# Even tokens first in every block, side taps of one chain alone, and a gate projected feature by token

## The chip, the cores and the metric

The kernel runs on one core of a Trainium2 chip. The metric is device time in microseconds (us) of one execution, from input in HBM to output in HBM. Engines are named as in the profile: PE is TensorE (matmuls; PEld its weight loads), DVE VectorE, ACT ScalarE, POOL GpSimd, SP SyncE, which issues all DMAs here.

## The reference

2048 tokens of 1024 features pass two residual layers and a last RMSNorm. Layer 0 is gated linear attention with 4 heads in chunks of 64 tokens, layer 1 a causal convolution module with 31 taps per channel. Each has a gate path z that multiplies the layer's output before its output projection. All is float32.

```python
def gla_mixer(h, w_in, w_g2, b_g, gn_w, w_out):          # layer 0
    q, k, v, z, g_lr = split(h @ w_in)
    log_a = log_sigmoid(g_lr @ w_g2 + b_g) / 16
    o = gla_chunked(q * dk**-0.5, k, v, log_a)            # state S, 64 tokens at a time
    o = o * rsqrt(mean(o * o) + EPS) * gn_w               # per head of 256
    return (o * silu(z)) @ w_out

def conv_mixer(h, w_in, dw_w, dw_b, ln_w, ln_b, w_out):   # layer 1
    a, gl, z = split(h @ w_in)
    u = causal_depthwise_conv(a * sigmoid(gl), dw_w) + dw_b   # 31 taps
    u = silu(layernorm(u, ln_w, ln_b))
    return (u * silu(z)) @ w_out

x = x + gla_mixer(rmsnorm(x), ...); x = x + conv_mixer(rmsnorm(x), ...); return rmsnorm(x)
```

## The kernel before

Work goes by two halves of 1024 tokens (`hf`), each in two blocks of 512 (`b`). Data lie with features on the 128 partitions and tokens along them. Every projection is three matmuls for one (`mm3`, L139 to 145): both operands are split into a high and a low part (`ah`/`al` for activations, `wh`/`wl` for weights, which ACT and POOL split in L124 and L125 as each unit of 256 columns arrives), and high x high, high x low and low x high are summed in a bank of PSUM. `proj_f` (L147) keeps 128 weight columns stationary and moves 512 tokens, so its result lies feature by token. `proj_t` (L152) keeps 128 tokens stationary and moves 256 weight columns, so its result lies token by feature. Eight row blocks make 24 matmuls in either.

Layer 0 (`head`, L442) goes head by head: q and k, the values v, then eight steps `i` of 128 tokens. A step projects z with `proj_t`, applies Silu on ACT (L472), and runs three parts of `core`: scores, `mix` (the output `o`, the state S) and `turn`. In `mix` the sum of squares gives a factor `ss`, and DVE multiplies o, ss and z into g (L403). `turn` transposes g back to feature by token on PE (L413); ACT copies it with the norm's weight (L418), and SP stores 256 tokens of it, read again by the output projection (`out1`).

Layer 1 (`in2`) projects a, gate and z of every unit. `glu` writes u = a * sigmoid(gate), with even tokens in `u[:, 0]` and odd ones in `u[:, 1]` (L754, a write in steps). `conv` splits the 31 taps into three filters of half length: A is 16 taps on even tokens, B 15 on odd ones, C 16 on even + odd. Even outputs are A plus B one token late, odd ones C - A - B, so 47 taps of 512 tokens stand for 62. On DVE a chain of taps is one multiply-add each (L638) into a bank of PSUM; its first tap also takes in what came before (L640 for C, L642 for A and B). The first `nside` taps of A and as many of B are done beside DVE: ACT multiplies (L622), POOL adds (L624). `SIDES` gives `nside` for each of eight chunks of 128 channels in both halves. POOL (in the first half) or DVE (in the second) forms even + odd in place (L669) once A is done. `even` (L647), `odd` (L652) and `sums` (L659) make the outputs and the sum for the layer norm. A layer norm of one half runs beside the projections of the next or beside `out2`, which adds the output projection to x (L838), sums squares (L844), scales (L864) and stores.

The order on each engine comes from a scheduler that plans with its own time line. The code sets priorities (`PRIO`), and `pump` (L588) doles out the list of conv and layer norm steps between projections. Pools set what waits: PSUM has three banks `mm` for projections, two `pb` for chains, three `pm`. Each engine works its queue in order.

Of the kernel before, what the change touches and what calls it, by code (L numbers as in the profile page):

```python
# [13 lines left out]
P = 128  # L14
# [16 lines left out]
SIDES = ((1, 7, 7, 7, 7, 5, 9, 7),  # L31
         (1, 5, 3, 5, 9, 7, 6, 4))
# [8 lines left out]
def kernel(  # L41
    ctx: ExitStack,
    tc: tile.TileContext,
    xT: bass.AP,
    wall: bass.AP,
# [21 lines left out]
    ps_m = ctx.enter_context(tc.tile_pool(name="ps_m", bufs=3, space=bass.MemoryType.PSUM))  # L67

# [70 lines left out]
    def mm3(ps, terms):  # L139
        n = len(terms)  # L140
        i = 0
        for sh, sl, mh, ml in terms:
            for s, m in ((sh, mh), (sh, ml), (sl, mh)):
                pe.matmul(ps, s, m, start=(i == 0), stop=(i == 3 * n - 1))  # L144
                i += 1

    def proj_f(ps, w, c0, a):  # L147

        wh, wl = w
        mm3(ps, [(wh[:, k, c0:c0 + P], wl[:, k, c0:c0 + P], a[k][0], a[k][1]) for k in range(KT)])  # L150
# [75 lines left out]
    wgr = l1c.tile([P, KT, 16], F32, name="wgr")  # L226

    masks = l1c.tile([P, 192], I32, name="masks")
# [9 lines left out]
    def load_small():  # L238
        sp.dma_start(out=wgr, in_=wg)
# [41 lines left out]
    def gate_low(hf, b, a, acc):  # L281
# [14 lines left out]
        rbs = t2("tmp")  # L296
        act.activation(rbs[0:96], rb[0:96], AF.Copy)
        gv = t2("tmp")
        dve.tensor_tensor(gv[0:96], ps[0:96], rbs[0:96], ALU.mult)
# [58 lines left out]
    late = []  # L358

# [5 lines left out]
    def core(hf, h, i, v, sz, qkb, sink):  # L365
# [11 lines left out]
        def scores():  # L377
# [3 lines left out]
            dve.copy_predicated(st[CK:P, CK:P], masks[CK:P, P:P + CK], s_ps[CK:P, P:P + CK])  # L381
# [3 lines left out]
        def mix():  # L385
# [17 lines left out]
            dve.scalar_tensor_tensor(g, o_ps, ss, sz, ALU.mult, ALU.mult)  # L403
            sink["g", i] = g

        def turn():
# [4 lines left out]
            for c in range(2):  # L411
                o = c * 256 + (i % 2) * P
                pe.transpose(gt[:, o:o + P], g[:, c * P:(c + 1) * P], ident)  # L413
            if i % 2 == 1:
                st = t2("st")
                for c in range(2):
                    cs = slice(c * 256, (c + 1) * 256)
                    act.activation(st[:, cs], gt[:, cs], AF.Copy, scale=cc(C_GN, 2 * h + c))  # L418
                if h < HEADS - 1:
                    for c in range(2):  # L420
                        r0 = (2 * h + c) * P
                        sp.dma_start(
                            out=gd[hf, r0:r0 + P, (i - 1) * P:(i + 1) * P],
                            in_=st[:, c * 256:(c + 1) * 256])
                else:
                    sink["stage"].append(st)
# [15 lines left out]
    def head(hf, h, a, EEs, g3s, stage):  # L442
# [23 lines left out]
        sink = {"stage": stage}  # L466
        todo = []
        for i in range(8):
            ps = mm_bank()[:, 0:DV]
            proj_t(ps, w, a[i // 4], i % 4)  # L470
            sz = l1p.tile([P, DV], F32, name="sz", bufs=3)
            act.activation(sz, ps, AF.Silu, scale=rt[:, hf * 8 + i:hf * 8 + i + 1])  # L472
            todo.append(core(hf, h, i, vs[i], sz, qkb[i // 4], sink))
# [20 lines left out]
    def out1(hf, stage, ahead):  # L494
        a = [[], []]
        for b in range(2):
            if b == 1:
                run_late(0)
            for k in range(KT):
# [6 lines left out]
                else:  # L506
                    for s in range(2):
                        src = stage[b * 2 + s][:, (k - 6) * 256:(k - 5) * 256]
                        ds = slice(s * 256, (s + 1) * 256)
                        act.activation(hi[:, ds], src, AF.Copy)  # L510
                        dve.tensor_tensor(lo[:, ds], src, hi[:, ds].bitcast(F32), ALU.subtract)
                a[b].append((hi, lo))
        accs = [l1p.tile([P, NB], F32, name="acc", bufs=2) for _ in range(2)]
        for pair in range(2):
            ws = [next_unit(12 + 2 * pair), next_unit(13 + 2 * pair)]
            for b in range(2):
                t0 = hf * TH + b * NB
                for ch in range(4 * pair, 4 * pair + 4):
                    xr = l1p.tile([P, 4, 3, CK], F32, name="Q", bufs=2).rearrange("p a b c -> p (a b c)")[:, 0:NB]
                    sp.dma_start(out=xr, in_=xT[ch * P:(ch + 1) * P, t0:t0 + NB])  # L520
# [77 lines left out]
    def conv(hf, c, u, dst, S1):  # L598
# [13 lines left out]
        def side(which):  # L612

            st[which] = l2p.tile([P, NB + 1], F32, name="conv" + which, bufs=2)
            acc = st["p" + which] = st[which][:, 1:NB + 1]
            for m in range(nside):
                src, w = tap(which, m)
                p = acc if m == 0 else l2p.tile([P, NB], F32, name="prod", bufs=2)
                if m == 0 and which == "B":
                    act.activation(p, src, AF.Identity, scale=w, bias=cc(C_DWB, c))  # L620
                else:
                    act.activation(p, src, AF.Copy, scale=w)  # L622
# [3 lines left out]
        def chain(which, m0, m1, n):  # L626
            def fn():
                first = 0 if which == "C" else nside
                if m0 == first:
                    st["ps"] = b_bank()  # L630
                ps = st["ps"]
# [19 lines left out]
        def odd():  # L651
            dve.scalar_tensor_tensor(  # L652
                dst[c][:, 1], st["ps"], dwb2[:, c:c + 1], st["B"][:, 1:NB + 1], ALU.add, ALU.subtract)
# [8 lines left out]
        for which, n in (("A", 16), ("B", 15), ("C", 16)):  # L662
            m0 = 0 if which == "C" else nside
# [324 lines left out]
```

## Time and profile before

| | |
|---|---|
| median of 3 runs | 1676.16 us (1675.92 to 1680.72) |
| profiled execution | 1678.1 us, span 1676.0 us |
| granted clock of PE, mean | 0.983 |
| PE, DVE, POOL, ACT busy | 96%, 58%, 54%, 44% of the span |
| DMA | 165.68 MB, 99 GB/s |

The span runs from the first to the last instruction in the trace. Layer 0 takes the first 860 us, the conv layer's input projections the time to 1445 us, and the last output projections the rest. Busy times of matmuls overlap, so PE's share is no measure of what it could do: the distance between the starts of two matmuls is. A wait is shown as the idle time before an instruction with what ended it.

### The profile page before, as it was taken

How to read it: one execution, taken by the hardware profiler on the slowest of the kernel's cores; microseconds unless marked ns; L12 is line 12 of the kernel's file. 1: busy time of each engine (PE TensorE's matmuls, PEld its weight loads, DVE VectorE, ACT ScalarE, POOL GpSimd, SP SyncE). 2: the span in 40 equal slices, each digit the busy share in tenths (PEclk: the TensorE clock that was granted, in tenths of full speed). 3: DMA queues.
4: the chain of work that ended last, by engine and by line, in shares of the span. 5: the costliest groups of instructions: out<-in, count | busy, mean ns of one | idle time of the engine just before them, and what ended most of it. 6: DMA issues, size and time to landing. Idle time of an engine off the chain costs nothing.

```text
span 1676.0 us, 23547 instructions
## 1 busy us (share of the span) xinstructions
PE 1609.4 (96%) x9028; PEld 1410.2 (84%) x9028; DVE 972.7 (58%) x1481; ACT 739.6 (44%) x1246; POOL 900.2 (54%) x787
## 2 busy tenths in 40 slices
PE   8999999999999999999999999999999899999697
PEld 6989999998889999999888887877788678877597
DVE  7433232241434232325243999989699999977634
ACT  6645252342557353415232544443553355435432
POOL 4444343334744333323342989985398798456342
PEclk9999999999999999999999999999999999999798
DMA  6021111144511212123452211225154113643633
GB/s 190 26 83 57 64 51 57 57 139 139 169 45 33 82 51 64 45 63 102 144 164 88 76 38 38 94 70 157 59 174 157 57 45 101 202 163 124 234 115 137
DMA packets 74016, 165.68 MB, mean 99 GB/s; under 512 B 7760, under 2 KB 16464, under 8 KB 73904
## 3 DMA queue, kind: packets, MB, share of 16 engines
q1 hardware_dynamic: 73904, 164.19, 30.5%
q8 instruction: 70, 1.15, 0.3%
q14 instruction: 42, 0.34, 0.1%
HBM read 128.51 MB, written 35.65 MB: 98 GB/s over the span
## 4 chain that ended last, share of the span: by engine, by line
PE 73%; DVE 16%; DMA 3%; ACT 3%; issue 2%; POOL 2%; SPq 0%; POOLq 0%; DVEq 0%; ACTq 0%
PE mm L144 63%; DVE pb L638 10%; PE pb L144 3%; PE pb L388 1%; PE pb L390 1%; DVE pb L642 1%; PE pm L379 1%; DMA wr<-in_wall_dram 1%; PE pm L413 1%; DVE u L754 1%; DVE al L190 1%; PE pm L288 1%; POOL acc L205 1%; DMA u<-x_scratch 1%; DVE pb L640 1%
## 5 line engine op out<-in xcount | busy, mean ns | idle before, releaser
L144 PE MATMUL mm<-ah,wh 128*128 128x512 f32 (+1 forms) x1600 | 595.3, 388 | 44.8 <-DVE u L838 20.4
L144 PE MATMUL mm<-al,wh 128*128 128x512 f32 (+1 forms) x1600 | 592.6, 385 | 0.0
L144 PE MATMUL mm<-ah,wl 128*128 128x512 f32 (+1 forms) x1600 | 590.0, 386 | 0.0
L125 POOL TENSOR_TENSOR wl<-wr,wh 128x1024 fp32r<-128x1024 f32 x140 | 344.0, 2471 | 214.9 <-ACT wh L124 208.9
L144 PEld LDWEIGHTS mm<-ah,wh 128*128 128x128 f32 x1600 | 302.3, 190 | 110.1 <-DVE u L838 20.0
L144 PEld LDWEIGHTS mm<-al,wh 128*128 128x128 f32 x1600 | 302.2, 190 | 57.1 <-issue 0.2
L144 PEld LDWEIGHTS mm<-ah,wl 128*128 128x128 f32 x1600 | 301.4, 190 | 58.0 <-issue 0.2
L144 PE MATMUL mm<-wh,ah 128*128 128x256 f32 x896 | 259.2, 289 | 0.0
L144 PE MATMUL mm<-wh,al 128*128 128x256 f32 x896 | 254.7, 284 | 0.0
L144 PE MATMUL mm<-wl,ah 128*128 128x256 f32 x896 | 254.2, 284 | 0.0
L124 ACT ACTIVATE wh<-wr 128x1024 fp32r<-128x1024 f32 x144 | 145.5, 1051 | 140.9 <-PE mm L144 92.4
L638 DVE SCALAR_TENSOR_TENSOR pb<-u,C,pb 128x512 f32<-128x512 f32 x252 | 184.9, 747 | 0.7
L638 DVE SCALAR_TENSOR_TENSOR pb<-u,dwc,pb 128x512 f32<-128x512 f32 x240 | 179.9, 750 | 1.2
L144 PEld LDWEIGHTS mm<-wl,ah 128*128 128x128 f32 x896 | 171.4, 191 | 0.4
L144 PEld LDWEIGHTS mm<-wh,ah 128*128 128x128 f32 x896 | 171.3, 191 | 0.4
L144 PEld LDWEIGHTS mm<-wh,al 128*128 128x128 f32 x896 | 171.3, 191 | 0.0
L622 ACT ACTIVATE prod<-u,C 128x512 f32<-128x512 f32 x148 | 105.5, 721 | 135.7 <-POOL convA L624 68.4
L624 POOL TENSOR_TENSOR convA<-convA,prod 128x512 f32<-128x512 f32 x74 | 98.3, 1329 | 5.7 <-ACT prod L622 1.6
L624 POOL TENSOR_TENSOR convB<-convB,prod 128x512 f32<-128x512 f32 x74 | 98.0, 1325 | 4.0 <-ACT convB L620 0.7
L397 DVE SCALAR_TENSOR_TENSOR S<-S,dec,pb 128x256 f32<-128x256 f32 x56 | 26.8, 479 | 95.4 <-PE pb L144 95.3
L401 POOL TENSOR_TENSOR ss<-ss,e 128x1 f32<-128x1 f32 x64 | 13.4, 209 | 124.4 <-ACT g L400 124.4
L523 DVE TENSOR_TENSOR Q<-mm,Q 128x512 f32<-128x512 f32 x32 | 22.1, 689 | 93.0 <-PE mm L144 78.3
(195 smaller groups left out, 2174.1 us busy)
## 6 DMA issues: line engine op xcount, KB each, us to landing
wr<-in_wall_dram SPq DMA_DIRECT2D x144, 512.0 KB, 4.1
raw<-in_xT_dram SPq DMA_DIRECT2D x32, 256.0 KB, 3.7
Q<-in_xT_dram SPq DMA_DIRECT2D x32, 256.0 KB, 3.2
x_scratch<-Q SPq DMA_DIRECT2D x32, 256.0 KB, 3.1
sz_scratch<-t SPq DMA_DIRECT2D x32, 256.0 KB, 2.3
b<-sz_scratch SPq DMA_DIRECT2D x32, 256.0 KB, 3.5
g_scratch<-st SPq DMA_DIRECT2D x48, 128.0 KB, 1.9
raw<-g_scratch SPq DMA_DIRECT2D x24, 256.0 KB, 3.5
```

Of the source, the lines that this page charges most:

```text
L124: act.activation(wh[:, ks, :], raw, AF.Copy)
L125: (dve if i < 2 else pool).tensor_tensor(wl[:, ks, :], raw, wh[:, ks, :].bitcast(F32), ALU.subtract)
L144: pe.matmul(ps, s, m, start=(i == 0), stop=(i == 3 * n - 1))
L190: dve.tensor_tensor(lo, src, hi.bitcast(F32), ALU.subtract)
L205: eng.tensor_tensor(acc, acc, sq, ALU.add)
L288: pe.matmul(ps, wgs[:, k, :], m, start=(n == 0), stop=(n == 15))
L379: pe.matmul(s_ps[:, 0:192], ki[:, js], Q[:, j].rearrange("p s c -> p (s c)"), start=True, stop=True)
L397: dve.scalar_tensor_tensor(S[h], S[h], dec[:, j:j + 1], kv, ALU.mult, ALU.add)
L523: dve.tensor_tensor(xr, ps, xr, ALU.add)
L622: act.activation(p, src, AF.Copy, scale=w)
L624: pool.tensor_tensor(acc, acc, p, ALU.add)
L638: dve.scalar_tensor_tensor(dstm, src, w, ps, ALU.mult, ALU.add)
```

## The change

1. Layer 0's z is projected with `proj_f`: 512 tokens move past 128 stationary columns, and one bank holds a pair of steps, filled half in each. DVE multiplies it with the row factor, ACT applies Silu in place. g is now o times `ss`, copied by ACT; the transposed g is multiplied with the norm's weight and z on DVE. One store carries 512 tokens.
2. The transposes write each pair of tokens apart, so from here on every block of 512 tokens lies with its 256 even tokens first. The residual input is given in this order (`xP`), the host puts the output back. u, the layer norm's product with z and others are then written and read in runs.
3. In `conv` only A has side taps (`SIDES` about doubled, 97 and 77 in place of 2 x 50 and 2 x 40), all into `convA`. The chains go B, A, C. B starts with a multiply and a bias add from one SBUF operand. A's sum stays in its bank of PSUM, from which `even` (now on DVE) reads it and C goes on. The sum even + odd is always on POOL.

The core of the diff:

```diff
-SIDES = ((1, 7, 7, 7, 7, 5, 9, 7),
-         (1, 5, 3, 5, 9, 7, 6, 4))
+SIDES = ((2, 14, 14, 14, 14, 10, 15, 14),
+         (2, 10, 6, 10, 15, 14, 12, 8))
...
+    def apart(t):
+
+        return t.rearrange("p (s t) -> p t s", s=2)
...
-            dve.scalar_tensor_tensor(g, o_ps, ss, sz, ALU.mult, ALU.mult)
+            act.activation(g, o_ps, AF.Copy, scale=ss)
...
             for c in range(2):
-                o = c * 256 + (i % 2) * P
-                pe.transpose(gt[:, o:o + P], g[:, c * P:(c + 1) * P], ident)
+                o = (i % 2) * CK
+                gv = gt[:, c * 256:(c + 1) * 256].rearrange("p (s t) -> p s t", s=2)[:, :, o:o + CK]
+                pe.transpose(gv.rearrange("p s t -> p t s"), g[:, c * P:(c + 1) * P], ident)
...
-                    act.activation(st[:, cs], gt[:, cs], AF.Copy, scale=cc(C_GN, 2 * h + c))
...
+                    dve.scalar_tensor_tensor(sv, gv, cc(C_GN, 2 * h + c), sv, ALU.mult, ALU.mult)
+                    if i % 4 == 3 and h < HEADS - 1:
                         r0 = (2 * h + c) * P
...
+                        sp.dma_start(out=gd[hf, r0:r0 + P, b * NB:(b + 1) * NB], in_=st)
...
         for i in range(8):
-            ps = mm_bank()[:, 0:DV]
-            proj_t(ps, w, a[i // 4], i % 4)
-            sz = l1p.tile([P, DV], F32, name="sz", bufs=3)
-            act.activation(sz, ps, AF.Silu, scale=rt[:, hf * 8 + i:hf * 8 + i + 1])
...
+            b, c = i // 4, i // 2 % 2
+            if i % 2 == 0:
+                ps = mm_bank()
+                proj_f(ps, w, c * P, a[b], range(0, 4))
+            else:
+                proj_f(ps, w, c * P, a[b], range(4, 8))
+                sz = sink["z", b, c] = t2("st")
+                dve.tensor_tensor(
+                    sz.rearrange("p (s t) -> p s t", s=2), ps.rearrange("p (t s) -> p s t", s=2),
+                    rbb[2 * hf + b].rearrange("p (s t) -> p s t", s=2), ALU.mult)
+                act.activation(sz, sz, AF.Silu)
...
-        def side(which):
+        def side():
...
                 for m in range(m0, m1):
                     src, w = tap(which, m)
-                    dstm = ps
-                    if m == n - 1 and which != "C":
-                        dstm = st["p" + which]
+                    dstm = st["B"][:, 1:NB + 1] if which == "B" and m == n - 1 else ps
                     if m > first:
                         dve.scalar_tensor_tensor(dstm, src, w, ps, ALU.mult, ALU.add)
-                    elif which == "C":
-                        dve.scalar_tensor_tensor(dstm, src, w, st["pA"], ALU.mult, ALU.subtract)
+                    elif which == "A":
+                        dve.scalar_tensor_tensor(dstm, src, w, st["pA"], ALU.mult, ALU.add)
+                    elif which == "B":
+                        dve.tensor_scalar(dstm, src, w, cc(C_DWB, c), ALU.mult, ALU.add)
                     else:
-                        dve.scalar_tensor_tensor(dstm, src, w, st["p" + which], ALU.mult, ALU.add)
+                        dve.scalar_tensor_tensor(dstm, src, w, ps, ALU.mult, ALU.subtract)
...
-            pool.tensor_tensor(d[:, 0], st["pA"], st["B"][:, 0:NB], ALU.add)
+            dve.tensor_tensor(d[:, 0], st["psA"], st["B"][:, 0:NB], ALU.add)
...
-        for which, n in (("A", 16), ("B", 15), ("C", 16)):
-            m0 = 0 if which == "C" else nside
+        for which, n in (("B", 15), ("A", 16), ("C", 16)):
+            m0 = nside if which == "A" else 0
...
             if which == "A":
-                items.append((0.0, lambda: (pool if hf == 0 else dve).tensor_tensor(ue, ue, uo, ALU.add)))
-            if which == "B":
-                items.append((0.0, even))
+                items.append((0.0, lambda: pool.tensor_tensor(ue, ue, uo, ALU.add)))
+                items.append((0.6, even))
...
-                zv = z.rearrange("p (t s) -> p s t", s=2)
+                zv = wide(z)
...
                 dve.tensor_tensor(
-                    u[:, :, o:o + 256].rearrange("p s t -> p t s"),
-                    a_ps.rearrange("p (t s) -> p t s", s=2),
-                    sg.rearrange("p (t s) -> p t s", s=2), ALU.mult)
+                    u[:, :, o:o + 256],
+                    a_ps.rearrange("p (s t) -> p s t", s=2),
+                    sg.rearrange("p (s t) -> p s t", s=2), ALU.mult)
```

DVE, first half, where C of the third chunk begins. Before: L652 ends the chunk before, L754 writes u of a later one, L640 is C's first tap. The last tap of A stands 17 instructions ahead of it.

```order
L638 SCALAR_TENSOR_TENSOR pb<-u,C,pb 128x512
L652 SCALAR_TENSOR_TENSOR d<-pb,dwb_96,convB 128x512
L754 TENSOR_TENSOR u<-mm,t_9744 128x256x2
L754 TENSOR_TENSOR u<-mm,t_9820 128x256x2
L638 SCALAR_TENSOR_TENSOR pb<-u,C,pb 128x512
L640 SCALAR_TENSOR_TENSOR pb<-u,dwc,convA 128x512
L638 SCALAR_TENSOR_TENSOR convB<-u,C,pb 128x512
```

Of the change, same place: L650 is A's first tap (it has two), L659 the even sum, L652 B's first tap of the next chunk, L654 C's first tap.

```order
L650 SCALAR_TENSOR_TENSOR pb<-u,C,convA 128x512
L648 SCALAR_TENSOR_TENSOR pb<-u,C,pb 128x512
L765 TENSOR_TENSOR u<-mm,t_8917 128x2x256
L648 SCALAR_TENSOR_TENSOR pb<-u,C,pb 128x512 x2
L648 SCALAR_TENSOR_TENSOR convB<-u,C,pb 128x512
L659 TENSOR_TENSOR d<-pb,convB 128x512
L652 TENSOR_SCALAR pb<-u,C 128x512
L648 SCALAR_TENSOR_TENSOR pb<-u,C,pb 128x512 x5
L654 SCALAR_TENSOR_TENSOR pb<-u,dwc,pb 128x512
```

C begins sooner after A: the taps of B that stood between them now stand ahead of A.

POOL, the same chunk's sum of even and odd u (L669 before, L681 after). Before: L624 are side adds, L125 a half of a weight unit's split.

```order
L624 TENSOR_TENSOR convB<-convB,prod 128x512
L125 TENSOR_TENSOR wl<-wr,wh 128x1024 x2
L796 COPY halo<-u 128x30
L624 TENSOR_TENSOR convB<-convB,prod 128x512 x4
L669 TENSOR_TENSOR u<-u 128x527
L624 TENSOR_TENSOR convA<-convA,prod 128x512 x5
```

Of the change: L636 are the side adds, L671 the sum for the layer norm, L127 the weight splits.

```order
L671 TENSOR_TENSOR S_8754<-d 128x1024
L687 COPY convB<-bcar 128x1
L636 TENSOR_TENSOR convA<-convA,prod 128x512
L127 TENSOR_TENSOR wl<-wr,wh 128x1024
L807 COPY halo<-u 128x30
L127 TENSOR_TENSOR wl<-wr,wh 128x1024
L681 TENSOR_TENSOR u<-u 128x527
L636 TENSOR_TENSOR convA<-convA,prod 128x512
```

Two splits now stand right ahead of the sum. Counted through the whole order, one or two stand right ahead of it in five of the sixteen chunks.

DVE in the last output projections. Before: L727 and L729 belong to the layer norm's second block, L190 splits y, L864 scales u of the first output block, L838 adds the projection to x of the third.

```order
L727 TENSOR_TENSOR d<-d,pm 128x2x256 x8
...
L864 SCALAR_TENSOR_TENSOR u<-u,C,pb 128x512 x2
L190 TENSOR_TENSOR al<-b_13830,ah 128x512
L864 SCALAR_TENSOR_TENSOR u<-u,C,pb 128x512 x4
L864 SCALAR_TENSOR_TENSOR prod<-prod,C,pb 128x512 x2
L844 TENSOR_TENSOR acc<-acc,pb 128x512
```

Of the change: L875 scales, L738 is the layer norm's second block, L849 adds the projection to x.

```order
L875 SCALAR_TENSOR_TENSOR u<-u,C,pb 128x512 x6
L855 TENSOR_TENSOR acc<-acc,pb 128x512
L875 SCALAR_TENSOR_TENSOR prod<-prod,C,pb 128x512 x2
L174 TENSOR_SCALAR v4n<-pm 128x4
L855 TENSOR_TENSOR acc<-acc,pb 128x512 x4
L738 TENSOR_TENSOR d<-d,pm 128x2x256 x8
L849 TENSOR_TENSOR u<-mm,u 128x512
```

The scaling now stands ahead of the layer norm's second block. On PE the broadcast of its factor stands 2 matmuls of 512 columns into the third output block, before 72; the broadcast for the layer norm's second block stands 58 into it, before at its start.

## Rows read from the trace of the kernel before

**Rows 1.** The page's first part: busy us, share of the span, instructions.
```profile
PE 1609.4 (96%) x9028; PEld 1410.2 (84%) x9028; DVE 972.7 (58%) x1481; ACT 739.6 (44%) x1246; POOL 900.2 (54%) x787
```
**Rows 2.** Windows: from:to, length, busy us (instructions) of PE, PEld, DVE, ACT, POOL; PE's clock; DMA.
```profile
200.00:400.00 200.00, 200.00 (x1329) 184.88 (x1328) 62.38 (x127) 73.93 (x160) 70.25 (x85) 1.00 0.26 81
...
1000.00:1190.00 190.00, 178.68 (x763) 145.65 (x762) 177.17 (x230) 84.91 (x121) 149.20 (x110) 0.97 0.28 89
1190.00:1445.00 255.00, 247.66 (x1087) 203.04 (x1086) 246.78 (x341) 126.86 (x177) 200.72 (x143) 0.99 0.33 106
1445.00:1490.00 45.00, 40.78 (x177) 32.46 (x176) 38.66 (x50) 13.56 (x17) 23.09 (x11) 1.00 0.62 203
...
1565.00:1582.00 17.00, 0.92 (x9) 0.73 (x7) 12.75 (x19) 6.13 (x10) 7.72 (x4) 0.64 0.81 278
```
**Rows 3.** The chain in order of time: start, us, engine, what, line, count.
```profile
581.28 14.39 PE mm L144 x120
...
810.24 57.84 PE mm L144 x255
```
**Rows 4.** Groups by line and shape: busy us, mean ns | idle before, what ended it.
```profile
L642 DVE SCALAR_TENSOR_TENSOR pb<-u,C,convB 128x512 f32<-128x512 f32 x16 | 26.5, 1654 | 5.2 <-POOL convB L624 5.2
L640 DVE SCALAR_TENSOR_TENSOR pb<-u,dwc,convA 128x512 f32<-128x512 f32 x16 | 26.0, 1626 | 0.0
L642 DVE SCALAR_TENSOR_TENSOR pb<-u,C,convA 128x512 f32<-128x512 f32 x16 | 21.3, 1331 | 0.9 <-ACT convA L622 0.9
L638 DVE SCALAR_TENSOR_TENSOR pb<-u,C,pb 128x512 f32<-128x512 f32 x252 | 184.9, 747 | 0.7
L754 DVE TENSOR_TENSOR u<-mm,t 128x512 f32<-128x512 f32 x32 | 33.2, 1071 | 22.8 <-PE mm L144 22.8
L838 DVE TENSOR_TENSOR u<-mm,u 128x512 f32<-128x512 f32 x12 | 8.0, 685 | 20.6 <-PE mm L144 14.2 <-DMA u<-x_scratch 6.5
L313 DVE TENSOR_SCALAR Ei<-pm,C 128x512 f32<-128x512 f32 x14 | 9.9, 746 | 2.7 <-ACT tmp L312 2.4
L669 DVE TENSOR_TENSOR u<-u 128x527 f32<-128x527 f32 x8 | 11.2, 1399 | 0.0
L729 DVE TENSOR_TENSOR b<-b,d 128x512 f32<-128x512 f32 x8 | 9.2, 1169 | 4.1 <-DMA b<-sz_scratch 4.1
L403 DVE SCALAR_TENSOR_TENSOR g<-pb,ss,sz 128x256 f32<-128x256 f32 x64 | 30.8, 482 | 53.7 <-POOL ss L402 53.5
L472 ACT ACTIVATE sz<-mm,rt 128x256 f32<-128x256 f32 x64 | 30.3, 474 | 55.3 <-PE mm L144 42.5 <-DVE g L403 12.1
L413 PE MATMUL pm<-ident,g 128*128 128x128 f32 x128 | 24.4, 272 | 0.0
```
**Rows 5.** Waits of PE from 900 to 1490 us: in total, times, longest.
```profile
PE mm L144 <- DVE u L754: 12.6, 6, 4.4
```
**Rows 6.** L640: ns min/median/max; and DVE's wait for POOL, 900 to 1490 us.
```profile
L640 DVE SCALAR_TENSOR_TENSOR pb<-u,dwc,convA x16: 746/1426/2893, 947.9 to 1458.0; 128x512 f32<-128x512 f32 x16
...
DVE pb L642 <- POOL convB L624: 5.2, 1, 5.2
```
**Rows 7.** POOL: a split in the time line; L669's ns min/median/max.
```profile
999.71 2.40 POOL L125 TENSOR_TENSOR wl<-wr,wh 128x1024 fp32r<-128x1024 f32 x1
...
L669 POOL TENSOR_TENSOR u<-u x8: 1330/1334/1787, 946.4 to 1140.1; 128x527 f32<-128x527 f32 x8
```
**Rows 8.** The end, time line of PE and DVE, and the chain: start, us.
```profile
1564.87 1.05 PE L178 MATMUL pb<-ident,r4f 128*128 128x128 f32 x8
1582.11 0.79 PE L144 MATMUL mm<-ah,wh 128*128 128x512 f32 x1 [16.19 <-DVE u L838]
...
1570.08 1.39 DVE L864 SCALAR_TENSOR_TENSOR u<-u,C,pb 128x512 f32<-128x512 f32 x2
...
1575.08 6.19 DMA u<-x_scratch
```

More of the change, by code (lines that the diff above doesn't have):

```diff
@@ L44 @@
     xT: bass.AP,
+    xP: bass.AP,
     wall: bass.AP,
@@ L137, in next_unit, with mm3 @@
         return wh, wl
-    def mm3(ps, terms):
+    def mm3(ps, terms, first=True, last=True):
         n = len(terms)
@@ L143, in mm3, with proj_f @@
             for s, m in ((sh, mh), (sh, ml), (sl, mh)):
-                pe.matmul(ps, s, m, start=(i == 0), stop=(i == 3 * n - 1))
+                pe.matmul(ps, s, m, start=(first and i == 0), stop=(last and i == 3 * n - 1))
                 i += 1
-    def proj_f(ps, w, c0, a):
+    def proj_f(ps, w, c0, a, ks=range(KT)):
         wh, wl = w
-        mm3(ps, [(wh[:, k, c0:c0 + P], wl[:, k, c0:c0 + P], a[k][0], a[k][1]) for k in range(KT)])
+        mm3(ps, [(wh[:, k, c0:c0 + P], wl[:, k, c0:c0 + P], a[k][0], a[k][1]) for k in ks],
+            0 in ks, KT - 1 in ks)
+    def apart(t):
+        return t.rearrange("p (s t) -> p t s", s=2)
     def proj_t(ps, w, a, j):
@@ L358 @@
     late = []
+    rbb = []
     def run_late(n):
@@ L411, in turn @@
             for c in range(2):
-                o = c * 256 + (i % 2) * P
-                pe.transpose(gt[:, o:o + P], g[:, c * P:(c + 1) * P], ident)
+                o = (i % 2) * CK
+                gv = gt[:, c * 256:(c + 1) * 256].rearrange("p (s t) -> p s t", s=2)[:, :, o:o + CK]
+                pe.transpose(gv.rearrange("p s t -> p t s"), g[:, c * P:(c + 1) * P], ident)
             if i % 2 == 1:
-                st = t2("st")
+                b, o = i // 4, (i % 4 // 2) * P
                 for c in range(2):
-                    cs = slice(c * 256, (c + 1) * 256)
-                    act.activation(st[:, cs], gt[:, cs], AF.Copy, scale=cc(C_GN, 2 * h + c))
-                if h < HEADS - 1:
-                    for c in range(2):
-                        r0 = (2 * h + c) * P
[L422 to L426, printed above, removed]
+                    st = sink["z", b, c]
+                    sv = st.rearrange("p (s t) -> p s t", s=2)[:, :, o:o + P]
+                    gv = gt[:, c * 256:(c + 1) * 256].rearrange("p (s t) -> p s t", s=2)
+                    dve.scalar_tensor_tensor(sv, gv, cc(C_GN, 2 * h + c), sv, ALU.mult, ALU.mult)
+                    if i % 4 == 3 and h < HEADS - 1:
+                        r0 = (2 * h + c) * P
+                        sp.dma_start(out=gd[hf, r0:r0 + P, b * NB:(b + 1) * NB], in_=st)
         return scores, mix, turn
@@ L506, in out1 @@
                 else:
[L507 to L511, printed above, removed]
+                    src = stage[2 * b + k - 6]
+                    act.activation(hi, src, AF.Copy)
+                    dve.tensor_tensor(lo, src, hi.bitcast(F32), ALU.subtract)
                 a[b].append((hi, lo))
@@ L610, in tap @@
             return ue[:, m:m + NB], dwc[:, c, m:m + 1]
-        def side(which):
-            st[which] = l2p.tile([P, NB + 1], F32, name="conv" + which, bufs=2)
-            acc = st["p" + which] = st[which][:, 1:NB + 1]
+        def side():
+            acc = st["pA"] = l2p.tile([P, NB], F32, name="convA", bufs=2)
             for m in range(nside):
-                src, w = tap(which, m)
+                src, w = tap("A", m)
                 p = acc if m == 0 else l2p.tile([P, NB], F32, name="prod", bufs=2)
[L619 to L622, printed above, removed]
+                act.activation(p, src, AF.Copy, scale=w)
                 if m > 0:
```

46 lines of the change are left out of this document (27 added, 19 removed).

## The prediction, made before the changed kernel ran

> **What bounds the kernel now.** I read the page first: TensorE (PE) is busy for 1609.4 of 1676.0 us, no other engine for more than 972.7 [rows 1]. That number hides stages, so the table of windows came next [rows 2]. From the start to 860 us (the GLA layer) PE has hardly a gap: 200.00 of 200.00 us in the second window, while VectorE (DVE), ScalarE (ACT) and GpSimd (POOL) are at 31, 37 and 35%. There only PE's own work counts. From 1000 to 1445 us (the conv layer's input projections) two engines are full: DVE 177.17 of 190 and 246.78 of 255 us, POOL 149.20 and 200.72, and PE still 178.68 and 247.66. [...] Last, from 1565 to 1582, PE does almost nothing (0.92 us) at a granted clock of 0.64: one wait of 16.19 us [rows 8].
>
> The pitch of matmuls is read from the chain, where a stretch of one kind follows without gaps [rows 3]: 120 of 256 columns in 14.39 us, 0.1199 us each; 255 of 512 columns in 57.84 us, 0.2268 each.
>
> **The change, part by part.**
>
> *1. The gate z of layer 0.* Two halves x 4 heads x 8 x 24 = 1536 matmuls of 256 columns become 768 of 512: 1536 x 0.1199 = 184.2 us against 768 x 0.2268 = 174.2, so **-10.0 us** [rows 3]. The work is in the stage where PE alone counts, so all of it shows.
>
> [...]
>
> What else moves in this stage is off PE. DVE loses 64 scalings of g (L403, 482 ns) and gets 32 products of z with the factor (0.69 to 1.07 us, by L838 and L754) and 64 of 256 columns (about 0.48): at most 34 us more in 840, beside an engine at 31%. ACT loses 64 Silu of 256 (L472, 474 ns) and 64 scaled copies, gets 32 Silu of 512 and 64 copies of g with a scale, some six table loads more: about even, at 37%. Both hidden [rows 2, 4]; if the cover were gone, PE would wait at the two banks that o and kv share, a few tenths of a us in 64 places. The gather into 512-token stores takes 16 DMAs off SP's queue; nothing waits for them until the output projection.
>
> *2. The transposes of g* write PSUM with even and odd tokens 128 words apart instead of in a run. 128 of them stand at 272 ns in the trace [rows 4]. No row shows PE writing in steps. From below 0 (PE makes as many columns as before). From above twice their pitch, which I bound by the 0.12 us of a 256-column matmul: 128 x 0.12 = 15.4 us [rows 3]. The nearest stepped write is DVE's L754, 1071 ns against 685 for L838 of the same size [rows 4], a factor 1.56. I take **+2**, near zero, since that one is an SBUF write by another engine.
>
> *3. DVE in the conv layer.* A chunk of 128 channels has 47 taps; before, n of A and n of B went to ACT and POOL, so DVE had 47 - 2n; now 47 - n. Over 16 chunks 752 - 180 = 572 become 752 - 174 = 578. What kind they are matters more. Of the 572, 524 read their second operand from PSUM (L638, 0.75 us) and 48 begin a chain with both operands in SBUF: L640 26.0 us, L642 26.5 and 21.3, in all 73.8 [rows 4]. L640's spread, 746 ns to 2893 [rows 6], shows that it is not slow by itself. After the change, C begins from the PSUM bank of A, B begins with one operand and two scalars, and only A's first tap has two in SBUF.
> So: 546 - 524 = 22 more fast taps, +16.5; the 48 first taps gone, -73.8; 16 of B at L313's 0.75, +12.0; 16 of A at L642's 1.33, +21.3; the even sum, now on DVE, 16 x 0.69 (L838), +11.0; the sum of even and odd u in the second half, now on POOL, -11.2 (L669); 32 writes of u in one run, 32 x (1.07 - 0.69) = -12.3; L729's eight products no longer stepped, about -2. The sum is **-38.5 us** of DVE, -12.7 in the first half and -25.8 in the second. [...] POOL gets ten side adds and eight sums of u more and sixteen even sums less: about even.
>
> *4. The new wait.* Before, B's taps stood between A's last tap and C's first, which covered the sum u = even + odd that C reads. Now B comes first, and the sum stands on POOL between A and C. Behind C's first tap everything on DVE is queued, the writes of u that free PE's banks too. In the first place shown with the change, six taps and the even sum are left as cover, 4.5 to 5 us; on POOL two weight splits (2.40 us each, [rows 7]) stand right ahead of the sum (1.33). Such splits stand right ahead in five of the sixteen chunks. Ends: 0 (in the eight chunks where the sum is on POOL today L640 never waited; POOL made DVE wait once, 5.2 us [rows 6]) and 16 x (2.40 + 1.33) = 60. I take one split uncovered in five places and 0.3 us in eleven: **+15**, nearer to what POOL's waits cost today.
>
> *5. The end.* The 16.19 us come so: the factor of the first output block is broadcast at 1564.87, DVE scales u from 1570.08, u is stored, and x of the next block comes into the same buffer at 1575.08 + 6.19 [rows 8]. Meanwhile PE has filled its three banks (72 matmuls) and stands. In the order before, that broadcast stands 72 matmuls into the third block; after it, 2. So the chain starts 70 x 0.227 = 15.9 us earlier against PE. What is late next: the first L838 of that block now stands behind eight L727, whose broadcast stands 58 matmuls into the block: 13.2 us + 8 x 0.69 = 18.7, while PE's banks are full at 16.3. Some 3 to 4 us of waiting stay, and the lower clock after them, and the last block's y is 13 us later than now. Ends: 0, and -16.2. I take **-10**, the wait less the 3 to 4 us and a little for the lower clock.
>
> **The sum.** -10.0 + 2 - 38.5 + 15 - 10 = -41.5. The profiled execution took 1678.1 us (span 1676.0), 1.9 over the median of 1676.16. 1678.1 - 41.5 = 1636.6; against the median **1635**.
>
> **Rivals.**
> *POOL sets the pace (slower).* The sum of u meets a pair of splits and its own time in every chunk: 2 x 2.40 + 1.33 = 6.1 us, 98 us instead of 15: 1635 + 83 = 1718. For it: POOL is at 79% in both windows, and a split waits for weights that wait for PE. Against: splits are right ahead in five chunks only, and POOL made DVE wait once. It decides from 56 / 16 = 3.5 us per chunk on.
> *DVE's time is hidden.* PE keeps its pace between 1000 and 1490, and another wait takes the place of the last one; only terms 1 and 2 are left, -8: 1668. For it: POOL paces the side taps and is as full as before. Against: PE's waits there are for DVE's writes.
> *Stepped transposes.* At twice the pitch: 15.4 instead of 2, 1648. [...]
> [...]
>
> **Chances.** Forecast 0.48, better 0.17, hidden 0.14, transposes 0.12, POOL 0.09. What lies within 0.3% (5 us) of 1676 can't be told from no change. Hidden lies next to that bound and gives 0.10 to faster; with forecast, better and transposes 0.86 or 0.87. Same 0.06, slower 0.08. The range from 1608 to 1668 leaves out POOL, the upper half of hidden and a little below better, 0.18.
>
> **What would show it.** Right: z's matmuls 0.227 us apart; C's first tap near 0.75 us and u's write near 0.69; PE's waits between 1000 and 1490 halved; no wait over 5 us in the last 110 us. Wrong: DVE idle before C's first tap for the sum of u, tens of us in all (term 4); transposes starts 0.2 us apart (2); first taps of B or A at 2 us (3); a wait of PE over 10 us near the end on another buffer (5).

## The result and the profile after

The changed kernel took 1657.97 us (median of 4 runs, 1655.97 to 1660.84) against 1676.04 beside it: a ratio of 0.9889, 95% interval 0.9863 to 0.9915. It is faster by 18 us where 41 were forecast. The profiled execution took 1656.6 us, its span is 1654.6.

The windows of the changed kernel, with the columns of [rows 2]:

```profile
1000.00:1190.00 190.00, 182.25 (x784) 147.88 (x783) 177.37 (x253) 88.72 (x127) 139.77 (x108) 0.98 0.28 89
1190.00:1445.00 255.00, 252.38 (x1129) 208.90 (x1128) 233.09 (x344) 127.03 (x174) 200.42 (x148) 1.00 0.36 118
...
1565.00:1582.00 17.00, 11.49 (x46) 8.88 (x45) 11.13 (x16) 5.91 (x9) 7.98 (x4) 0.77 0.35 126
```

In the conv layer's two windows PE does 63 matmuls more in the same time. From 1565 to 1582 it works for 11.49 us instead of 0.92. But the first layer ended no earlier. The inverse norm that follows its last output projection starts at the same time as before (time line of PE, first of the kernel before, then of the changed one):

```profile
867.92 0.95 PE L166 MATMUL pm<-ones,acc 128*128 128x1 f32 x8
```
```profile
868.64 0.95 PE L173 MATMUL pm<-ones,acc 128*128 128x1 f32 x8
```

To add this up I took from each trace the distance from every matmul's start to the next, less the median of its kind (227 ns at 512 columns, 120 at 256 in the projections), and summed it over three stretches: up to that inverse norm, from there to the layer norm's first mean of the second half (L693, now L704), and to the end. This is PE's lost time, waits and lower clock together, in us. (Behind the wait of 16.19 us in [rows 8], for one, matmuls of 512 columns start 0.43 us apart until 1586.5 us, at a granted clock of 0.50 from 1582 to 1585; from 1587 on they start 0.227 apart at 1.00.)

| | first layer | conv layer | end | span |
|---|---|---|---|---|
| before | 17.7 | 34.6 | 31.0 | 1676.0 |
| changed | 28.0 | 19.5 | 23.1 | 1654.6 |
| z alone | 28.4 | 35.7 | 32.8 | 1679.7 |
| the rest alone | 17.6 | 21.5 | 13.8 | 1645.3 |

The changed kernel lost 10.3 us more in the first layer, 15.1 less in the conv layer and 7.9 less at the end; matmuls themselves took 8.7 less. Together that is -21.4, the difference of the spans. The level of the first column depends on the choice of kinds: with one median for each shape alone it reads 29.0 before and 39.2 changed. The differences between the rows then move by 0.4 us at most.

What PE waited for from 930 to 1490 us (line waited for: us, times, longest). Before, besides the 12.6 us of [rows 5]:

```profile
PE mm L144 <- DVE u L838: 4.2, 4, 1.8
PE mm L144 <- ACT t L767: 3.1, 1, 3.1
PE mm L144 <- ACT t L750: 3.0, 2, 2.4
```

In the changed kernel:

```profile
PE mm L146 <- ACT t L778: 4.1, 3, 2.8
PE mm L146 <- ACT t L761: 3.5, 3, 1.9
PE mm L146 <- DVE u L849: 2.9, 1, 2.9
PE pm L704 <- POOL S L671: 2.7, 1, 2.7
```

The waits for the write of u are all gone. PE waited 16.8 us for DVE before and 2.9 now; 7.6 us for ACT and 2.7 for POOL are left beside it.

The groups by shape in the changed kernel, to be read against [rows 4]:

```profile
L654 DVE SCALAR_TENSOR_TENSOR pb<-u,dwc,pb 128x512 f32<-128x512 f32 x16 | 12.0, 751 | 10.1 <-POOL u L681 10.1
L650 DVE SCALAR_TENSOR_TENSOR pb<-u,C,convA 128x512 f32<-128x512 f32 x16 | 19.1, 1195 | 0.5 <-POOL convA L636 0.5
L652 DVE TENSOR_SCALAR pb<-u,C 128x512 f32<-128x512 f32 x16 | 12.9, 806 | 0.2
L765 DVE TENSOR_TENSOR u<-mm,t 128x512 f32<-128x512 f32 x32 | 21.3, 684 | 25.0 <-PE mm L146 23.4 <-ACT t L761 1.4
L425 PE MATMUL pm<-ident,g 128*128 128x128 f32 x128 | 24.4, 272 | 0.0
```

C's first tap takes 0.751 us instead of 1.626, B's 0.806 instead of 1.654, the write of u 0.684 instead of 1.071. The wait that the change adds is the 10.1 us on C's first tap. The transposes take 272 ns, as before, and the two of a step start 109 ns apart in both kernels.

What PE waits for in the first layer, 0 to 930 us of the changed kernel (line waited for: us, times, longest):

```profile
PE pm L295 <- ACT ah L277: 6.9, 1, 6.9
PE mm L146 <- DVE Q L539: 3.8, 2, 2.7
PE mm L146 <- DVE vl L447: 2.7, 2, 1.4
PE pm L360 <- POOL kd L354: 1.9, 2, 1.0
```

The first is the start of the program, also there before. The other three are six waits at 77, 236, 380, 512, 671 and 817 us, 8.4 us in all, none of which the kernel before has. Behind the last, of 2.7 us, the next eight matmuls take 3.46 us from start to start instead of 1.82, at a granted clock of 0.50 from 820 to 822 us: 1.6 us of lower clock. Behind the other five, of 0.95 to 1.38 us, the clock is 1.00. One of them, and what was there before, on ACT's time line (start, us, then the instruction; vh is the value that PE's bank waits to be split). The changed kernel, then the one before:

```profile
225.54 1.28 ACT L326 ACT_TABLE_LOAD   x1
226.84 0.63 ACT L326 ACTIVATE tmp<-tmp 128x512 f32<-128x512 f32 x1
227.37 0.67 ACT L322 ACTIVATE tmp<-pm,C 128x512 f32<-128x512 f32 x1
228.06 1.28 ACT L328 ACT_TABLE_LOAD   x1
...
230.01 1.28 ACT L326 ACT_TABLE_LOAD   x1
...
232.31 1.28 ACT L328 ACT_TABLE_LOAD   x1
...
236.75 0.46 ACT L446 ACTIVATE vh<-mm,r 128x256 fp32r<-128x256 f32 x1
```
```profile
227.96 1.28 ACT L316 ACT_TABLE_LOAD   x1
229.26 1.15 ACT L316 ACTIVATE tmp<-tmp 128x512 f32<-128x512 f32 x2
230.43 1.28 ACT L318 ACT_TABLE_LOAD   x1
231.72 1.15 ACT L318 ACTIVATE tmp<-tmp 128x512 f32<-128x512 f32 x2
```

Before, the gate's exponential (L316) runs for both blocks of tokens, then the logarithm (L318). In the new order the second block comes in late, and the two alternate: two loads of ACT's function tables (ACT_TABLE_LOAD, 1.28 us each) more, and PE stands 1.4 us for the value behind them. The wait at 817 is another chain (chain of waits of the changed kernel):

```profile
811.68 4.28 DMA x_scratch<-Q
...
816.01 3.15 DMA Q<-in_xP_dram
...
819.29 0.70 DVE Q L539
...
820.04 2.08 PE mm L146 x4
```

The residual x of the output projection comes into one of two buffers, which must be stored before it is loaded again; PE waits for the add that empties its bank.

The end of the changed kernel, PE's waits from 1490 us:

```profile
PE mm L146 <- DVE d L849: 4.2, 2, 4.1
PE mm L146 <- ACT wh L126: 4.0, 1, 4.0
PE pb L173 <- DVE acc L855: 2.6, 1, 2.6
...
PE mm L146 <- DVE u L849: 1.6, 1, 1.6
PE mm L146 <- POOL wl L127: 1.5, 1, 1.5
```

The 16.19 us of [rows 8] are gone. The add that the forecast had late next is the one into u, the first of the third output block: it stands behind the layer norm's L738 (chain of waits), and PE waits 1.6 us for it.

```profile
1552.12 1.79 DVE d L738 x3
1553.92 0.24 DVE u L849
```

The 4.1 us are an add of the second block, into d. The kernel before has such a wait too (its waits of PE from 1490 to 1600 us):

```profile
PE mm L144 <- DVE d L838: 3.5, 1, 3.5
```

New is a weight unit (L126, L127) that comes late, 5.5 us with nothing like it in the forecast.

### The profile page after: what moved, and what is told of

The parts are those of the page before. It is cut to its first block, busy times and chain, and to the rows that moved or that the text cites. A ratio compares the mean times of both kernels' runs of the same rounds, so it can differ in the third digit from the quotient of the medians.

```text
span 1654.6 us, 22003 instructions
## 1 busy us (share of the span) xinstructions
PE 1596.6 (96%) x8260; PEld 1366.6 (83%) x8260; DVE 963.1 (58%) x1519; ACT 735.8 (44%) x1206; POOL 890.4 (54%) x789
## 4 chain that ended last, share of the span: by engine, by line
PE 76%; DMA 7%; DVE 6%; ACT 5%; issue 3%; POOL 2%; SPq 0%; POOLq 0%; DVEq 0%; ACTq 0%
PE mm L146 67%; PE pb L146 2%; DVE al L197 2%; PE pb L399 1%; DMA wr<-in_wall_dram 1%; PE pb L401 1%; PE pm L390 1%; DMA raw<-x_scratch 1%; DMA Q<-in_xP_dram 1%; ACT d L739 1%; DVE pb L648 1%; DMA x_scratch<-Q 1%; PE pm L295 1%; PE pm L425 1%; POOL wl L127 1%
## 5 line engine op out<-in xcount | busy, mean ns | idle before, releaser
L146 PE MATMUL mm<-ah,wh 128*128 128x512 f32 (+1 forms) x1856 | 698.3, 389 | 30.4 <-ACT wh L126 4.7
L146 PE MATMUL mm<-al,wh 128*128 128x512 f32 (+1 forms) x1856 | 692.9, 386 | 0.0
L146 PE MATMUL mm<-ah,wl 128*128 128x512 f32 (+1 forms) x1856 | 691.1, 386 | 1.5 <-POOL wl L127 1.5
L127 POOL TENSOR_TENSOR wl<-wr,wh 128x1024 fp32r<-128x1024 f32 x140 | 341.8, 2457 | 247.8 <-ACT wh L126 241.9
L146 PEld LDWEIGHTS mm<-ah,wl 128*128 128x128 f32 x1856 | 348.9, 189 | 69.1 <-POOL wl L127 2.3
L636 POOL TENSOR_TENSOR convA<-convA,prod 128x512 f32<-128x512 f32 x158 | 207.7, 1316 | 12.0 <-ACT prod L634 5.2
L126 ACT ACTIVATE wh<-wr 128x1024 fp32r<-128x1024 f32 x144 | 145.7, 1051 | 141.0 <-PE mm L146 91.9
L634 ACT ACTIVATE prod<-u,C 128x512 f32<-128x512 f32 x158 | 112.7, 721 | 113.2 <-POOL convA L636 112.7
L146 PE MATMUL mm<-wh,ah 128*128 128x256 f32 x384 | 109.2, 284 | 0.0
L146 PE MATMUL mm<-wl,ah 128*128 128x256 f32 x384 | 109.1, 284 | 0.0
L146 PE MATMUL mm<-wh,al 128*128 128x256 f32 x384 | 108.9, 284 | 0.0
L146 PEld LDWEIGHTS mm<-wl,ah 128*128 128x128 f32 x384 | 73.6, 192 | 0.4
L146 PEld LDWEIGHTS mm<-wh,ah 128*128 128x128 f32 x384 | 73.5, 192 | 0.3
L146 PEld LDWEIGHTS mm<-wh,al 128*128 128x128 f32 x384 | 73.6, 192 | 0.1
```

What stands on the lines that cost most here:

```text
L126: act.activation(wh[:, ks, :], raw, AF.Copy)
L127: (dve if i < 2 else pool).tensor_tensor(wl[:, ks, :], raw, wh[:, ks, :].bitcast(F32), ALU.subtract)
L146: pe.matmul(ps, s, m, start=(first and i == 0), stop=(last and i == 3 * n - 1))
L636: pool.tensor_tensor(acc, acc, p, ALU.add)
```

## The experiments

Each ran beside the kernel before (medians 1675.3 to 1677.9 us); times are medians, waits and stretches are of one profiled execution. Every edit gives the scheduler a new plan, and that moves waits far from the edit. Among the runs of the changed kernel that leave its first layer's code as it is, that layer ended between 867.0 and 869.8 us (873.2 with chains A, B, C), and the end lost 17 to 38 us. A difference of a few us of the whole time is therefore no proof of one cause.

**z alone.** The layer-0 part in the old token order, the conv layer as before.

```diff
-                    u[:, :, o:o + 256],
+                    u[:, :, o:o + 256].rearrange("p s t -> p t s"),
 (likewise the transposes, the store of g, x, conv and SIDES of the kernel before)
```

> Only part 1 of the change: z by 512 columns, in the old token order; conv layer as before. In the changed kernel the first layer ends no earlier than before (868.6 us against 867.9, by the inverse norm after its output projection), though z should save 10. Theory W (the new order of ACT, DVE and SP in this layer brings some 12 us of new waits of PE, and they come with z itself): 1674 to 1678 us, first layer ends at 866 to 869. Rival S (the waits come from the even-first writes and loads): 1665 to 1669 us, first layer ends at 857 to 860.

1682.9 us, ratio 1.0036 (1.0023 to 1.0050): by itself this part makes the kernel slower. The first layer ends at 868.7 us. The same six waits are there, in the old token order. Theory W holds on where they come from; the time is above both ranges, since the later stages lost some us more as well.

**The rest alone.** The changed kernel with z by token as before.

```diff
-                proj_f(ps, w, c * P, a[b], range(0, 4))
...
+            ps = mm_bank()[:, 0:DV]
+            proj_t(ps, w, a[i // 4], i % 4)
+            act.activation(sz, ps, AF.Silu, scale=rt[:, hf * 8 + i:hf * 8 + i + 1])
...
-            act.activation(g, o_ps, AF.Copy, scale=ss)
+            dve.scalar_tensor_tensor(g, o_ps, ss, sz, ALU.mult, ALU.mult)
...
-                    dve.scalar_tensor_tensor(sv, gv, cc(C_GN, 2 * h + c), sv, ALU.mult, ALU.mult)
+                    act.activation(sv, gv, AF.Copy, scale=cc(C_GN, 2 * h + c))
```

> The changed kernel with z by token as before (1536 matmuls of 256 columns, Silu and product as before), even-first order, conv and tail as changed. Theory W: z is worth nothing net, so 1656 to 1661 us, first layer ends at 866 to 870. Rival S: the waits stay and the 10 us of pitch come back on top, so 1666 to 1671 us, first layer ends near 878.

1647.1 us (1644.6 to 1649.9), ratio 0.9824 (0.9807 to 0.9840): faster than both kernels. The first layer ends at 867.4, none of the six waits is left. That is theory W. Below the expected range it comes by its end: 9.3 us less lost there. 5.5 of them are the wait for weights, which it does not have, and 2.4 a shorter wait for the add into d (waits of PE from 1490 us):

```profile
PE pb L173 <- DVE acc L847: 3.9, 2, 2.6
PE mm L146 <- DVE d L841: 2.1, 2, 1.7
...
PE mm L146 <- DVE u L841: 1.6, 1, 1.6
```

**Transposes in one run.**

```diff
-                pe.transpose(gv.rearrange("p s t -> p t s"), g[:, c * P:(c + 1) * P], ident)
+                pe.transpose(gt[:, o:o + P], g[:, c * P:(c + 1) * P], ident)
...
-                    gv = gt[:, c * 256:(c + 1) * 256].rearrange("p (s t) -> p s t", s=2)
+                    gv = gt[:, c * 256:(c + 1) * 256].rearrange("p (t s) -> p s t", s=2)
```

> The changed kernel with the 128 transposes written in one run as before; the product on DVE reads PSUM in steps in their place. Theory (stepped transposes cost PE nothing): their pitch stays at 0.11 us and the time within 3 us of the changed kernel, 1655 to 1661. Rival (they cost up to 0.12 us each): 1643 to 1650.

1655.5 us (1650.2 to 1656.6), within the theory's range. The transposes take 272 ns and start 109 ns apart here too; DVE's product reads PSUM in steps at 477 ns, the same as in a run.

**Fewer taps,** in the changed kernel and in the one before.

```diff
-        for which, n in (("B", 15), ("A", 16), ("C", 16)):
+        for which, n in (("B", 14), ("A", 16), ("C", 15)):
```

> The changed kernel without the last tap of B and of C in every chunk: 32 taps of 0.748 us, 24 us less on DVE, left out of the computation. Theory D (DVE still sets PE's waits from 1000 to 1490 us): PE gets 10 to 17 us, 1641 to 1648. Rival P (what is left of the waits there is ACT's and POOL's order, DVE is no longer last): 1653 to 1659.

> The kernel before without the last tap of B and of C in every chunk: 32 taps of 0.747 us, 24 us less on DVE, left out of the computation. How much of DVE's time reaches the end in the kernel before? Theory (a half to three quarters, as in the changed kernel, where 24 us gave 18): 1657 to 1664 us. [...] Rival N (less than a third, since other waits take over at once): 1668 to 1676.

(The edit as in the changed kernel; in the one before the order stays A, B, C.) The changed kernel: 1640.1 us, 18 less for 24 us of DVE, just below theory D's range. PE's lost time in the conv layer and at the end falls from 42.6 to 27.7. But the mechanism is mixed. PE waited for no write of u in the changed kernel either; what went are 4.5 us for weights at the end, 2.3 for POOL's sum S, 1.5 for ACT and 2.6 for adds of DVE, 10.9 of the 14.9; the other 4.0 are in none of these (mean granted clock 0.990 against 0.988). Its waits of PE from 930 to 1460 us, after which an add at 1471 us costs 5.3:

```profile
PE mm L146 <- ACT t L778: 3.1, 2, 1.6
PE mm L146 <- ACT t L761: 3.1, 1, 3.1
PE pm L704 <- POOL S L671: 0.4, 1, 0.4
```

The kernel before: 1663.0 us against 1677.9, ratio 0.9917 (0.9902 to 0.9931), 15 less for the same 24. Lost time in the two stretches falls from 65.6 to 53.7, and all of that is at the end (31.0 to 11.5), where the wait of 16 us does not come up in this order. The conv layer lost more than with all taps, 42.2 us instead of 34.6: PE still waits 13.5 us for the write of u, and 14.2 for ACT instead of 6.1. The time lies in the theory's range. But that a share of 60 to 75% of DVE's time reaches the end in either kernel is not shown: in the one most of the waits that went were for other engines, in the other it is one gap that the new order leaves out.

**Chains A, B, C** with the side taps as changed.

```diff
-        for which, n in (("B", 15), ("A", 16), ("C", 16)):
+        for which, n in (("A", 16), ("B", 15), ("C", 16)):
 (the even sum moves behind B)
```

> The changed kernel with the old order of chains, A, B, C, the side taps still in A alone. B's 15 taps (11 us) then stand between A and C and cover POOL's sum of even and odd u, for which DVE waited 10.1 us in 6 places. Theory (that wait reaches PE at about half, as the 24 us of DVE did in the run with fewer taps): 1651 to 1655 us, C's first tap waits under 1 us. Rival (A has nothing ahead of it now, and its first tap waits for up to 14 side adds of 1.31 us on POOL instead): 1660 to 1675, tens of us of DVE waiting for convA.

1702.6 us, ratio 1.0152 (1.0130 to 1.0174): neither. DVE does not wait for the sum of u, and 0.3 us for convA, yet the conv layer loses 69.1 us. The largest piece is at 1487 us, where x of the output projection comes late (wait of PE from 1480 to 1515):

```profile
PE mm L146 <- DVE u L850: 22.7, 1, 22.7
```

The chain of waits through it:

```profile
1504.63 0.77 DVE pb L648
1505.41 4.02 DMA u<-x_scratch
...
1509.53 0.70 DVE u L850
```

DVE is still at its taps until 1505, and x can only be loaded when they free a buffer of u. Why DVE is this far behind in that order I did not follow further; with 44.6 us over the changed kernel it costs more than any single term of the forecast.

**z in one piece,** all 24 matmuls of a pair at the first of its two steps.

```diff
-                proj_f(ps, w, c * P, a[b], range(0, 4))
+                proj_f(ps, w, c * P, a[b])
...
-                proj_f(ps, w, c * P, a[b], range(4, 8))
```

> The changed kernel with all 24 matmuls of a pair's z at its first step, not 12 at each. Theory W2 (the 10 us of new waits in the first layer are those of PE running ahead of chains that do not get shorter: second block of q and k, values after the gate, residual loads): they stay in about the same places, first layer ends at 867 to 870, 1655 to 1661 us. Rival (they come from z's bank being held open over two steps): first layer ends at 859 to 862, 1647 to 1651.

1654.7 us (1650.4 to 1658.3), by the theory within 0.3 us, first layer to 868.1, the six waits in their places. A bank held open over two steps is not what makes them.

**Three product buffers.**

```diff
-                p = acc if m == 0 else l2p.tile([P, NB], F32, name="prod", bufs=2)
+                p = acc if m == 0 else l2p.tile([P, NB], F32, name="prod", bufs=3)
```

> The changed kernel with three product buffers for the side taps instead of two, so that ACT may run one product further ahead of POOL's adds. PE's waits from 930 to 1490 us are by now for ACT in 7.6 of 13.2 us (sigmoid of the gate, Silu of z), and ACT waits 112.7 us behind POOL's adds. Theory (ACT comes late because it stands behind a product that waits for POOL): those 7.6 us halve, 1650 to 1655. Rival (POOL's adds pace ACT all the same, a buffer more only shifts the wait): 1656 to 1661.

1660.8 us (1658.5 to 1666.3): the rival. PE's waits for ACT are 8.6 us instead of 7.6; ACT still stands 94.5 us behind POOL's adds (112.7 before).

**Weights first** at the end.

```diff
-                w = next_unit(28 + u)
+                with tc.high_priority(offset=PRIO):
+                    w = next_unit(28 + u)
```

> The changed kernel with the output projection's weight units (load and split) at the projections' priority. In the changed kernel PE stood 4.0 us for ACT and 1.5 for POOL at 1572 us, weights that the planner had put behind the layer norm's last splits; the kernel with the rest alone had no such wait and a tail 9.6 us shorter. Theory (that place in the order is the reason): 1648 to 1653 us. Rival (DVE's or the loads' lateness only moves to the next matmuls): 1655 to 1661.

1656.2 us (1653.9 to 1658.0): PE's waits for weights at the end shrink from 5.5 to 2.3 us and this stretch loses 17.2 us instead of 23.1, but the conv layer loses 3.0 more and the first layer 1.6, and PE's waits for the adds into u at the end grow from 1.6 to 4.6 us. By its time this is the rival, and no gain that can be told from none.

**The sum of u in its own buffer,** in the changed kernel and in the rest alone.

```diff
-            return ue[:, m:m + NB], dwc[:, c, m:m + 1]
+            return st["us"][:, m:m + NB], dwc[:, c, m:m + 1]
...
-        items = []
+        def both():
+            st["us"] = l2p.tile([P, HALO + NB], F32, name="us", bufs=1)
+            pool.tensor_tensor(st["us"], ue, uo, ALU.add)
+
+        items = [(0.0, both)]
...
-                items.append((0.0, lambda: pool.tensor_tensor(ue, ue, uo, ALU.add)))
```

> The changed kernel with the sum of even and odd u written to a buffer of its own, so that POOL can form it before A is done; the order of chains stays B, A, C. Theory (the new wait of C's first tap, 10.1 us of DVE in 6 places, costs PE half to three quarters of it): the wait is gone, 1650 to 1653 us. Rival (DVE's lateness has other covers): 1656 to 1660.

> The kernel with the rest alone (z by token as before; 1647.1 us) and the sum of u in a buffer of its own. Theory as for the sum's own buffer in the changed kernel: 1639 to 1643 us. Rival: 1645 to 1649.

1668.1 us (ratio 0.9947, 0.9927 to 0.9968) and 1649.8, the first above both ranges, the second just above the rival's. The edit did not take the wait away: DVE still waits 6.6 and 7.3 us for the sum (10.1 and 8.4 with the sum in place), since POOL does it when its turn comes. The conv layer loses 20.7 and 18.2 us instead of 19.5 and 21.5. So what this wait costs stays open. The 10 us more in the first of the two are at the end: out's store, x's load into the same buffer and the add make PE wait again, as in [rows 8] (PE's waits from 1490 us):

```profile
PE mm L146 <- DVE u L852: 12.0, 1, 12.0
```

**Without the log,** in the changed kernel and in the rest alone.

```diff
-            act.activation(ab, ab, AF.Ln, bias=1.0)
+            act.activation(ab, ab, AF.Exp)
```

> The changed kernel with the logarithm of the gate replaced by a second exponential (the log is left out of the computation): ACT loads its table 34 times instead of 58. Theory (the waits of PE at 77, 236, 512 and 671 us, 5.2 us in all, are ACT's gate chain, two of them because exponential and logarithm of two blocks alternate with a table load of 1.28 us each): they go, first layer ends at 862 to 865, 1651 to 1655 us. Rival (PE runs into the next thing that did not get shorter): first layer ends at 867 to 869, 1656 to 1660.

> The kernel with the rest alone (z by token, 1647.1 us) with the logarithm of the gate replaced by a second exponential (left out of the computation), as in the run without the log of the changed kernel, which gained 5.3 us and ended its first layer at 860.4 instead of 868.6. Theory I (with z by token ACT's gate chain is covered by PE's work, and only z by 512 bares it): 1645 to 1649 us, first layer ends at 866 to 868. Rival (the shorter chain gains the same in both): 1640 to 1643, first layer ends at 859 to 862.

In the changed kernel 1652.7 us, as the theory had it, and the first layer ends 8.2 us earlier, before the theory's 862 (time line of PE):

```profile
860.43 0.95 PE L173 MATMUL pm<-ones,acc 128*128 128x1 f32 x8
```

The four waits at 77, 236, 512 and 671 us are gone, those for x at 380 and 817 stay (waits of PE from 0 to 930 us):

```profile
PE mm L146 <- DVE Q L539: 4.7, 2, 3.4
```

In the rest alone 1644.6 us (1640.2 to 1646.9), and the first layer ends 2.8 us earlier, at 864.6. That lies between theory I's range and the rival's. ACT's gate chain is nearly covered with z by token, and bare with z by 512 columns: 5.4 of the 8.2 us are theory I's, the other 2.8 the rival's.

**x in its own buffers.**

```diff
-                    xr = l1p.tile([P, 4, 3, CK], F32, name="Q", bufs=2).rearrange("p a b c -> p (a b c)")[:, 0:NB]
+                    xr = t2("tmp")
```

> The changed kernel with the residual x of the first output projection in three buffers of the gate's (free by then) instead of the two that hold q, so that its loads need not wait for the last scores. Theory (PE's waits at 380 and 817 us, 1.3 and 2.9 us and 1.9 of lower clock, are loads of x that come late): they go, first layer ends at 862 to 865, 1651 to 1655 us. Rival (the adds wait for the last head's g anyway): 867 to 869 and 1656 to 1660.

1669.6 us (ratio 0.9947, 0.9927 to 0.9967), above both ranges: the waits at 380 and 817 are gone, but those buffers are the gate's, and the next half's start now stands behind them (waits of PE from 430 to 500 us):

```profile
PE pm L173 <- POOL acc L212: 8.0, 2, 5.6
PE pm L320 <- DVE g L312: 3.3, 1, 3.3
```

The first layer ends at 882.8. That the two waits were loads of x is shown; what they are worth is not.

## Why the prediction was wrong

The direction was right and most terms came out; the size was not: 18 us instead of 41. On the profiled executions the miss is 1656.6 - 1636.6 = 20 us: 10.3 of new lost time with z and 1.3 in the matmuls themselves, 8.4 in the conv layer, 2.1 at the end, less the 2 that the transposes did not take. The time lies in the stated range of 1608 to 1668, but two terms of the sum did not do what was forecast of them.

*Term 1, the gate z.* The pitch is right: in the first layer matmuls took 9.6 us less (867.9 - 17.7 = 850.2 before, 868.6 - 28.0 = 840.6 after; -10.0 forecast). The step that failed stands behind it: "Both hidden [rows 2, 4]; if the cover were gone, PE would wait at the two banks that o and kv share, a few tenths of a us in 64 places." I took the engines' busy shares of 31 to 37% for cover. PE does wait, not at those banks but at six other places, for chains that pass through several engines and did not get shorter with z: the gate's exponential, logarithm and scan, and load, add and store of x. The one shown at 237 us got longer, by two table loads. New lost time is 10.3 us; what z saves is eaten whole. z alone and the rest alone show that these waits come with z, and the runs without the log that four of the six are ACT's gate chain. This is half of the miss. Two things are not shown: how much of it comes from PE being done sooner and how much from the new order of ACT's and DVE's work that came with z, and whether another order could keep the 10 us; z in one piece did not.

*Term 2, the stepped transposes.* +2 was taken, 0 measured: 272 ns before and after [rows 4], starts 109 ns apart in both, and 1655.5 us with a run in their place. The rival at twice the pitch falls for these transposes of 128 float32 columns.

*Term 3, DVE.* The work is right: the taps, sums and writes of u that the term lists add up to 511.3 us before and 473.0 after, 38.3 less where 36.5 were forecast for them; the other 2, L729's eight products, did not come (9.4 us before, 11.3 after). The step that failed is the one from DVE's time to PE's: the sum books all 38.5 us at the end, and no run shows that so much of DVE's time reaches it. PE lost 15.1 us less where 23.5 were forecast for terms 3 and 4; this is 8.4 us of the miss. Of PE's waits from 930 to 1490 us, 22.9 in all, 16.8 were for DVE, and 13.9 of these went; ACT's did not (6.1 before, 7.6 now), and 2.7 for POOL's sum came up. Which part of the lighter DVE took the waits for u away is not shown: the kernel before with 24 us of taps left out kept them (13.5 us). The first tap of A, with both operands in SBUF, still takes 1.195 us; there are 16 such taps now instead of 48.

*Term 4, the new wait.* +15 was forecast, 10.1 us of DVE's waiting measured, in 6 of 16 places, at most 4.0. The rival in which POOL sets the pace falls. How much of the 10.1 us reaches the end is not shown, since the runs with the sum in its own buffer kept most of the wait.

*Term 5, the end.* -10 forecast, 7.9 less lost. The wait of 16.19 us went as worked out. The add that is late next costs 1.6, where 3 to 4 stood; the term's own figures, 18.7 against 16.3, give 2.4. The weight unit that ACT and POOL split too late, 5.5 us, was not foreseen. The kernel with z by token has the same code there and no such wait: its place is the scheduler's choice.

Of the rivals none came out. 1658 lies between the forecast and the one in which DVE's time is hidden (1668), but the mechanism is another: DVE's time showed in part, and z's did not at all.

## What to carry to other kernels

An engine that is idle for two thirds of the time is no proof of cover: before a saving on the bounding engine is booked, follow the longest chain through the others between two of its needs, with table loads and transfers in it, and compare it with the work of the bounding engine that lies beside it after the saving. What a faster engine can give the bounding one is what that one waits for it (here 16.8 of 22.9 us of waits), and the lower clock where the trace has it behind a wait (1.6 us behind one of 2.7 us, none behind five of 0.95 to 1.38), so list the waits by what ended them before pricing. A run with a known piece left out needs the same look: 24 us of taps gave 15 and 18 us here, but in good part through other engines' waits and a new order. A change of several parts should be run in parts: here z gave nothing in its own layer, and without it the kernel is 11 us faster, nearly all of that at the end, where the code is the same and only the scheduler's order differs.

## What was not expected of the hardware

DVE reading PSUM in steps of two words took 477 ns for 128 x 256, as long as in a run; the stepped write to SBUF had cost 1071 against 684. ACT's table load took 1.28 us each time; where exponential and logarithm alternated over two blocks, two loads, 2.56 us, came on top of those of the kernel before.
